# Softmax attention on one Trainium2 core: products of P and V read 232 columns in place of 256

## The chip, the cores and the metric

The kernel runs on one core of a Trainium2 chip. The metric is the device time of one execution in microseconds (us). Before the change it is 2531.12 us, the median of three runs that lie between 2529.14 and 2533.62 us.

## The reference

Two layers work on 1040 frames (16 learned ones and 1024 of the input) of width 1024. Each layer normalises, projects to a group of four gated-linear-attention heads and a group of eight softmax-attention heads of width 64, normalises both outputs by head, projects them back and adds them; then comes a gated feed-forward part with a short causal convolution. The change touches the softmax heads alone:

```python
c = jnp.cumsum(log_f, axis=1)
logits = einsum('bqhd,bkhd->bhqk', q_b * dh ** -0.5, kf) + c_b[..., None] - c_k[:, :, None, :]
logits = jnp.where(key_pos[None, :] <= q_pos[:, None], logits, -jnp.inf)
out = einsum('bhqk,bkhd->bqhd', jax.nn.softmax(logits, axis=-1), vf)
```

Everything is float32. The kernel keeps most operands of its matmuls as two parts, a rounded high one (`hi`, type float32r) and the rest (`lo`), and adds the products of the parts.

## The kernel before

The softmax attention is in `fox` (L770). The 1040 frames are cut into nine tiles: tile 0 has 112 frames (`FIRST`), the others 116 (`FT`). The eight heads are worked on as four pairs `p`, each with two heads `e`. For each pair the query tiles come in the groups (7, 8), (5, 6), (3, 4), (1, 2) and (0). One step of `fox` is one query tile of one head, and steps are laid out in slots:

- `fox_scores` (L644) multiplies queries with keys in up to three stretches of keys (460, 464 and 116 columns; L659 with the high part of the keys, L660 with the low one) into score buffers `S`, of which there are three. VectorE adds the gate's bias and takes the running minimum (L662), ScalarE takes the exponential into `P` (L674).
- Two slots later `fox_transposes` (L681) turns blocks of P on TensorE (L695; L688 for the ninth key tile), and `split` (L336 on ScalarE, L337 on VectorE) writes the high and low parts into `PT`. `PT[0]` holds key tiles 0 to 3, `PT[1]` key tiles 4 to 7, each as 4 places of 232 columns: the two query tiles of the group side by side. Key tile t stands at place `p = 3 - t % 4`, so key tiles 0 and 4 stand last.
- Three slots later `fox_av` (L699) multiplies V with PT into one buffer `av` (L721), 128 rows (high and low part of V, 64 each) by the group's 232 columns. Each key tile gives two matmuls, with the high and the low part of PT, and the same 116 x 128 (or 112 x 128) block of V as the stationary operand. Key tiles that only the later query tile may see are multiplied with 116 columns.
- Later slots fold the two halves of `av` (`fo`, L734), normalise, and store.

Between these steps `work.run` puts matmuls of other work as a filling: the projections of the next head pair and the gate branch (`mm`, L222 to L224, 348 or 344 columns), and for the last pair the output projection (`mm` of 256, 384 and 400 columns). How much goes into a slot is set by `mm_us` (L132), a cost for each matmul that doesn't change here. Within attention the order on each engine is then set by a scheduler, which goes by the order in the program, by its own costs of the instructions, and by a priority that `fox` gives to the scores (L818). In the feed-forward part the order on TensorE is written out by hand.

Of the kernel before, what the change touches and what calls it, by code (L numbers as in the profile page):

```python
# [33 lines left out]
FT, NT, FIRST = 116, 9, 112  # L34
# [101 lines left out]
class Kern:  # L136
# [562 lines left out]
    def fox_av(self, e, tiles, q, PT, avs, pp, part):  # L699
        nc = self.nc  # L700
        if part == 0:
            PT["av"] = pp.tile([128, 256], F32, tag="av", name="av")
        av = PT["av"]
        last = tiles[-1]
        width = FT * (len(tiles) - 1) + self.rows_of(last)
        ts = list(range(4 * part, min(4 * part + 4, last + 1)))
        if part == 0 and last:
            ts[:2] = 1, 0
        for t in ts:
            a, b = 0 if t <= tiles[0] else FT, width  # L710
            for i in range(2):
                if t == NT - 1:
                    w, x = q["Vm"][:, e, :, :], PT[2][:, i, :]
                else:
                    r, p = self.rows_of(t), 3 - t % 4
                    w, x = q["V"][e][:r, t, :, :], PT[part][:r, i, p, a:width]
                    if a == 0 and p < 3:

                        b = 256
                        x = PT[part][:r, i].rearrange("p a b -> p (a b)")[:, 2 * FT * p:2 * FT * p + b]  # L720
                nc.tensor.matmul(av[:, a:b], w.rearrange("p a b -> p (a b)"), x,  # L721
                                 start=(t == ts[0] and part == 0 and i == 0), stop=(t == last and i == 1))
        if last < 4 * part + 4:
            nc.scalar.copy(avs[:, e, :width], av[:, :width])
# [1024 lines left out]
```

## Time and profile before

| | before |
|---|---|
| time, median of three runs | 2531.12 us |
| the profiled execution's own time | 2528.19 us |
| its span, first to last instruction | 2526.4 us |
| mean granted clock of TensorE | 0.996 |
| TensorE busy | 2488.1 us |
| VectorE, ScalarE, GpSimd busy | 1767.5, 1274.1, 381.4 us |
| products of P and V, first and last start over both layers | 189.5 and 1753.7 us |

A row of the groups reads: line, engine, operation, what it writes and reads, rows times columns of the stationary operand, rows times columns of the moving one, count, then busy time in us, mean of one in ns, and idle time before it. A row of the timeline reads: start in us, duration, engine, line, operation, names, shape, how many follow each other under the same names, with the shape of the first; in brackets the idle time before it. A row of stretches reads: from and to, length, busy time and count of each engine in the order that the text names, granted clock, share of the DMA engines, GB/s.

### The profile page before, as it was taken

The numbers are of one execution on the slowest core, as the hardware profiler recorded it, in microseconds if no ns is written. First come the engines' busy times: TensorE is split into PE (matmuls) and PEld (weight loads), VectorE is DVE, ScalarE is ACT, GpSimd is POOL, SyncE is SP. The second block draws the span as 40 slices with busy tenths as digits, with TensorE's granted clock in tenths as the row PEclk, the third lists the DMA queues.
The fourth block names the chain that finished last, engine by engine and source line by source line (L and its number), as shares of the span: only waits on it lengthen the run. The fifth ranks groups of instructions, "written<-read, shape, count | busy, mean of one in ns | idle before, by whom it ended". The sixth has DMA issues, their size and how long they took to land.

```text
span 2526.4 us, 47023 instructions
## 1 busy us (share of the span) xinstructions
PE 2488.1 (98%) x18454; PEld 2386.5 (94%) x18454; DVE 1767.5 (70%) x3515; ACT 1274.1 (50%) x2731; POOL 381.4 (15%) x561
## 2 busy tenths in 40 slices
PE   9999999999999999999999999999999999999998
PEld 8989999999999999999999899999999999997786
DVE  8656777769877777853666666777797777777545
ACT  7346666645544445641443466665464444455412
POOL 1023433110000000100200333431100000001002
PEclk9999999999999999999999999999999999999999
DMA  3232124342322224763312222243432222258622
GB/s 131 68 87 73 50 89 132 116 139 76 118 81 81 81 76 138 196 176 102 105 56 70 74 80 69 67 147 110 145 92 93 76 82 83 77 158 191 183 75 73
DMA packets 117933, 259.75 MB, mean 103 GB/s; under 512 B 14816, under 2 KB 32480, under 8 KB 117712
## 3 DMA queue, kind: packets, MB, share of 16 engines
q1 hardware_dynamic: 93408, 181.74, 23.1%
q0 software_dynamic: 22432, 72.71, 10.4%
q8 instruction: 144, 2.36, 0.4%
q10 hardware_dynamic: 1872, 2.31, 0.3%
q14 instruction: 77, 0.63, 0.1%
HBM read 176.11 MB, written 67.81 MB: 97 GB/s over the span
## 4 chain that ended last, share of the span: by engine, by line
PE 83%; DVE 10%; ACT 4%; issue 1%; DMA 1%; SPq 0%; DVEq 0%; ACTq 0%
PE up L224 11%; PE up L222 11%; PE up L223 11%; PE mm L222 7%; PE mm L224 7%; PE mm L223 7%; PE down L222 5%; PE down L223 5%; PE down L224 5%; PE av L721 3%; PE tr L695 2%; DVE S L662 1%; PE S L659 1%; PE wo L222 1%; PE wo L224 1%
## 5 line engine op out<-in xcount | busy, mean ns | idle before, releaser
L224 PE MATMUL up<-x,hi 128*128 128x260 f32 (+1 forms) x2464 | 698.0, 283 | 2.8 <-DVE x L1090 2.8
L222 PE MATMUL up<-x,hi 128*128 128x260 f32 (+1 forms) x2464 | 698.2, 283 | 2.4 <-ACT x L1089 2.4
L223 PE MATMUL up<-x,lo 128*128 128x260 f32 (+1 forms) x2464 | 697.1, 283 | 0.0
L224 PEld LDWEIGHTS up<-x,hi 128*128 128x128 f32 x2464 | 466.8, 189 | 5.1 <-DVE x L1090 4.8
L222 PEld LDWEIGHTS up<-x,hi 128*128 128x128 f32 x2464 | 465.7, 189 | 3.3 <-ACT x L1089 3.2
L223 PEld LDWEIGHTS up<-x,lo 128*128 128x128 f32 x2464 | 466.0, 189 | 0.1
L1066 DVE TENSOR_TENSOR lo<-raw,hi 128x512 fp32r<-128x512 f32 x364 | 247.5, 685 | 172.0 <-ACT hi L1065 172.0
L222 PE MATMUL mm<-xh,hi 128*128 128x348 f32 (+4 forms) x1056 | 363.6, 344 | 0.0
L224 PE MATMUL mm<-xl,hi 128*128 128x348 f32 (+4 forms) x1056 | 339.6, 322 | 0.0
L223 PE MATMUL mm<-xh,lo 128*128 128x348 f32 (+4 forms) x1056 | 338.9, 321 | 0.0
L1065 ACT CAST hi<-raw 128x512 fp32r<-128x512 f32 x364 | 224.8, 620 | 141.5 <-PE up L224 93.0
L222 PEld LDWEIGHTS mm<-xh,hi 128*128 128x128 f32 x1056 | 199.6, 189 | 5.9 <-issue 5.3
L223 PEld LDWEIGHTS mm<-xh,lo 128*128 128x128 f32 x1056 | 199.5, 189 | 0.4 <-issue 0.3
L224 PEld LDWEIGHTS mm<-xl,hi 128*128 128x128 f32 x1056 | 198.4, 188 | 0.4 <-issue 0.3
L189 ACT CAST hi<-raw 128x512 fp32r<-128x512 f32 (+2 forms) x168 | 97.3, 580 | 183.2 <-PE down L224 108.0
L223 PE MATMUL down<-ah,lo 128*128 128x260 f32 (+1 forms) x528 | 169.1, 320 | 0.0
L222 PE MATMUL down<-ah,hi 128*128 128x260 f32 (+1 forms) x528 | 168.6, 319 | 0.0
L224 PE MATMUL down<-al,hi 128*128 128x260 f32 (+1 forms) x528 | 168.4, 319 | 0.0
L674 ACT ACTIVATE P<-S,m 116x460 f32<-116x460 f32 (+2 forms) x224 | 124.7, 561 | 71.6 <-DVE m L662 67.6
L337 DVE TENSOR_TENSOR PT<-tr,PT 116x464 fp32r<-116x464 f32 (+3 forms) x240 | 122.8, 514 | 47.0 <-ACT PT L336 45.4
L1048 DVE TENSOR_TENSOR raw<-raw,raw 128x512 f32<-128x512 f32 x198 | 129.4, 683 | 18.1 <-DMA raw<-in_wd_dram 15.6
L1279 POOL DMA_DIRECT2D actd<-cv x44 | 23.6, 535 | 763.0 <-DVE cv L1278 742.1
(285 smaller groups left out, 5615.6 us busy)
## 6 DMA issues: line engine op xcount, KB each, us to landing
raw<-in_wm_dram SPq DMA_DIRECT2D x326, 256.0 KB, 2.7
raw<-in_wd_dram SPq DMA_DIRECT2D x64, 256.0 KB, 3.8
actd<-cv POOLq DMA_DIRECT2D x22, 520.0 KB, 3.0
actd<-cv POOLq DMA_DIRECT2D x22, 512.0 KB, 3.0
cb<-cd SPq DMA_DIRECT2D x16, 520.0 KB, 4.2
st<-actd SPq DMA_DIRECT2D x14, 520.0 KB, 5.0
st<-actd SPq DMA_DIRECT2D x14, 512.0 KB, 4.8
kA<-kA SPq DMA_DIRECT2D x24, 260.0 KB, 4.1
```

The source lines that it names most:

```text
L189: nc.scalar.copy(hi[:, :n, :], raw[:, :n, :])
L222: nc.tensor.matmul(ps, wh, xh[:, c0:c0 + n], start=first, stop=False, skip_group_check=more)
L223: nc.tensor.matmul(ps, wl, xh[:, c0:c0 + n], start=False, stop=False, skip_group_check=more)
L224: nc.tensor.matmul(ps, wh, xl[:, c0:c0 + n], start=False, stop=last, skip_group_check=more)
L337: nc.vector.tensor_tensor(out=lo, in0=src, in1=hi.bitcast(F32), op=ALU.subtract)
L659: nc.tensor.matmul(S[:rows, :n], q["qA"][e][:, qs], q["kA"][e][:, c0:k1], start=True, stop=False)
L674: nc.scalar.activation(P[:rows, :n], S[:rows, :n], AF.Exp, scale=-1.0, bias=m[:rows, nch - 1:nch], accum_out=(den if nch == 1 else d3[:row ...
L695: nc.tensor.transpose(tr[:w, 3 - j, :rows], P[:rows, o:o + w], id_)
L721: nc.tensor.matmul(av[:, a:b], w.rearrange("p a b -> p (a b)"), x, start=(t == ts[0] and part == 0 and i == 0), stop=(t == last and i == 1))
L1048: nc.vector.tensor_tensor(out=q[out][:, :nk, :], in0=q[a][:, :nk, :], in1=q[b][:, :nk, :], op=op)
L1065: nc.scalar.copy(hi[:, :nk, :], src[:, :nk, :])
L1066: nc.vector.tensor_tensor(out=lo[:, :nk, :], in0=src[:, :nk, :], in1=hi[:, :nk, :].bitcast(F32), op=ALU.subtract)
```

## The change

Where a product reads both query tiles' columns (`a == 0`) of a key tile that doesn't stand last in PT (`p < 3`), the kernel before reads 256 columns in place of 232. The 24 additional ones are the beginning of the next place of PT; their products land in columns 232 to 255 of `av`, which nothing reads. After the change, every such product reads the 232 columns that it needs.

```diff
                 else:
                     r, p = self.rows_of(t), 3 - t % 4
                     w, x = q["V"][e][:r, t, :, :], PT[part][:r, i, p, a:width]
-                    if a == 0 and p < 3:
-
-                        b = 256
-                        x = PT[part][:r, i].rearrange("p a b -> p (a b)")[:, 2 * FT * p:2 * FT * p + b]
                 nc.tensor.matmul(av[:, a:b], w.rearrange("p a b -> p (a b)"), x,
                                  start=(t == ts[0] and part == 0 and i == 0), stop=(t == last and i == 1))
```

## The prediction

> **What bounds the kernel now.** I read four views: the page's first part for how full each engine is, its chain for which engine sets the end, the table by stretches for the two attention stages that the change touches, and the waits of TensorE there.
>
> ```profile
> span 2526.4 us, 47023 instructions
> ...
> PE 2488.1 (98%) x18454; PEld 2386.5 (94%) x18454; DVE 1767.5 (70%) x3515; ACT 1274.1 (50%) x2731; POOL 381.4 (15%) x561
> ...
> PE 83%; DVE 10%; ACT 4%; issue 1%; DMA 1%; SPq 0%; DVEq 0%; ACTq 0%
> ```
> ```profile
> 188.00:502.00 314.00, 309.40 (x2177) 298.83 (x2177) 224.68 (x712) 204.63 (x619) 105.21 (x158) 0.99 0.30 92
> 1440.00:1756.00 316.00, 311.48 (x2188) 300.28 (x2187) 225.72 (x716) 206.41 (x624) 105.33 (x158) 0.99 0.31 92
> ```
> ```profile
> PE mm L224 <- DVE ml L337: 1.7, 1, 1.7
> PE S L659 <- ACT P L674: 1.3, 3, 0.7
> PE av L721 <- ACT PT L336: 0.3, 1, 0.3
> PE av L721 <- DVE PT L337: 0.3, 1, 0.3
> PE tr L695 <- DVE PT L337: 0.3, 1, 0.3
> ```
>
> TensorE is busy for 98% of the span and holds 83% of the chain that ended last. In the two attention stages (second fence; the columns behind the length are TensorE, its weight loads, VectorE, ScalarE and GpSimd) it is busy 309.4 of 314 us and 311.5 of 316 us, while VectorE and ScalarE are busy 65 to 72% of the time. The third fence, the waits of the first attention stage from 188 to 480 us, adds up to under 4 us, and only 0.6 us of them stand before a product of P and V. So a nanosecond taken from TensorE's stream in these stages is a nanosecond off the end, unless a wait takes its place.
>
> **The change part by part.** It removes columns, and no instruction. In the table of groups, with shapes kept apart, the products of P and V with 128 columns of V stand in these three widest forms:
>
> ```profile
> L721 PE MATMUL av<-PT,V 116*128 116x256 f32 x448 | 96.7, 291 | 0.7 <-ACT PT L336 0.7
> L721 PE MATMUL av<-PT,V 112*128 112x232 f32 x128 | 24.8, 275 | 0.0
> L721 PE MATMUL av<-PT,V 116*128 116x232 f32 x64 | 13.5, 288 | 0.5 <-DVE PT L337 0.5
> ```
>
> The first row is what changes: 448 matmuls read 256 columns and will read 232, like the 192 of the two rows below (those of the first key tile of each four, `p = 3`, which have nothing behind them to read). In the built program of the changed kernel all 640 have 232. The mean of one (291 ns against 275 and 288) is latency and overlaps its neighbours; what a matmul costs is the distance from its start to the next start. The timeline gives it where eight stand together, two of 232 columns and then six of 256. Each run below is quoted as its start, the start of its third matmul, and the start of what follows:
>
> ```profile
> 270.54 1.10 PE L721 MATMUL av<-PT,V 116*128 116x232 f32 x8
> 270.76 0.87 PE L721 MATMUL av<-PT,V 116*128 116x256 f32 x6
> 271.47 0.26 PE L695 MATMUL tr<-ident,P 116*116 116x116 f32 x1
> 281.06 1.10 PE L721 MATMUL av<-PT,V 116*128 116x232 f32 x8
> 281.28 0.88 PE L721 MATMUL av<-PT,V 116*128 116x256 f32 x6
> 281.99 0.26 PE L695 MATMUL tr<-ident,P 116*116 116x116 f32 x1
> 352.18 1.10 PE L721 MATMUL av<-PT,V 116*128 116x232 f32 x8
> 352.41 0.88 PE L721 MATMUL av<-PT,V 116*128 116x256 f32 x6
> 353.12 0.26 PE L695 MATMUL tr<-ident,P 116*116 116x116 f32 x1
> ```
> ```profile
> 278.91 0.28 PE L721 MATMUL av<-PT,V 116*128 116x256 f32 x1
> 279.03 0.38 PE L660 MATMUL S<-kL,qA 128*116 128x460 f32 x1
> 279.25 0.28 PE L721 MATMUL av<-PT,V 116*128 116x256 f32 x1
> 279.37 0.26 PE L695 MATMUL tr<-ident,P 116*116 116x116 f32 x1
> ```
>
> Six of 232 take 0.22 + 0.22 + 0.23 = 0.67 us, 0.112 us each. Eighteen of 256 take 3 x 0.71 = 2.13 us, 0.118 us each; single ones (second fence) take 0.12. The difference is 0.0066 us by the runs and 0.0083 by the singles. A wider lever is the slope over columns, from the output projection's matmuls of 256 and 384 columns:
>
> ```profile
> 457.20 0.27 PE L222 MATMUL mm<-mh,hi 128*128 128x256 f32 x1
> ...
> 458.14 0.27 PE L224 MATMUL mm<-ml,hi 128*128 128x256 f32 x1
> ...
> 472.24 0.33 PE L222 MATMUL mm<-mh,hi 128*128 128x384 f32 x1
> ...
> 473.28 0.34 PE L222 MATMUL mm<-mh,wl 128*128 128x384 f32 x1
> ```
>
> From 457.20 to 458.14 stand eight intervals of 256 columns, 0.1175 us each; from 472.24 to 473.28 six of 384, 0.1733 us each. That is 0.436 ns a column, so 24 columns would be 10.5 ns. Over 448 matmuls the three prices are 3.0, 3.7 and 4.7 us. I take 7.8 ns, 3.5 us, between the first two, since these rows are of the very instruction; 4.7 us stays as the far end and nothing as the near one.
>
> Against this saving speaks the weight load that goes with each matmul. The rows above put a product of 232 columns at 0.112 us. [...]
>
> What moves: the instructions are the same, but the scheduler sees shorter matmuls and orders anew. Of 18,131 rows of TensorE 38 stand elsewhere, 128 of 3,517 on VectorE, 64 of 2,506 on ScalarE, 10 on GpSimd and 2 on SyncE (two loads of the gate branch that change places with a weight load, in a queue that TensorE waits for nowhere in the fence of waits). On TensorE nearly all of it is one place, the first query pair of head pair 0, once a layer: seven projection matmuls (`mm`, 348 columns) that stood between products and transposes now come behind them, ahead of the fold. On VectorE and ScalarE a split of transposed P or a score reduction steps past one or two neighbours. This is where a new wait can come from, so I look at that stretch:
>
> ```profile
> 189.50:204.20 14.70, 13.15 (x97) 11.73 (x95) 10.30 (x33) 11.36 (x35) 3.59 (x6) 1.00 0.00 1
> ```
> ```profile
> 194.00:198.00 4.00, 2.97 (x22) 1.00 0.00 0
> ```
> ```profile
> 205.56 0.32 PE L222 MATMUL mm<-xh,hi 128*128 128x348 f32 x1
> 205.72 0.32 PE L223 MATMUL mm<-xh,lo 128*128 128x348 f32 x1
> ```
>
> TensorE idles 14.70 - 13.15 = 1.55 us there, 1.03 of it between 194 and 198 us, where it waits for the softmax (scores for a free score buffer). A projection matmul takes 0.16 us. If the stretch is held by the softmax chain, the seven no longer fill its holes and come on top: 7 x 0.16 = 1.12 us a layer. If it is held by TensorE, moving them costs nothing; and two of them sat where the new order has products with their operands ready, which could shorten the idle time by as much. ScalarE is busy 11.36 of 14.70 us there, TensorE 13.15, so I take the latter, at nothing, and keep 2 x 1.12 = 2.2 us on either side. VectorE's and ScalarE's steps past a neighbour are hidden by the projection matmuls that stand between a transpose and the product that reads it; where these are gone is the stretch just priced.
>
> The sum: -3.5 + 0 = -3.5 us. The profiled execution took 2528.2 us (its span 2526.4 and 1.8 around it) and would take 2524.7; it lies 2.9 us under the median of the three runs, 2531.1, from which the forecast is 2527.6.
>
> **The rivals.** First, the clock makes it more. In both layers TensorE loses half its clock shortly after its longest wait:
>
> ```profile
> 454.60:458.40 3.80, 2.05 (x18) 1.85 (x18) 3.80 (x16) 3.80 (x12) 0.26 (x1) 1.00 0.21 71
> 458.40:461.80 3.40, 3.40 (x19) 3.40 (x18) 3.40 (x11) 3.40 (x10) 0.97 (x3) 0.50 0.52 155
> ```
>
> After 1.75 us of idleness in 3.8 us the granted clock is 0.50 for 3.4 us, a loss of 1.7 us. [...] Against it: nothing makes the wait itself shorter.
>
> Second, the other side. The first query pair becomes a longer hole: the seven matmuls no longer fill it, 1.12 us are added, and the 1.03 us of idleness between 194 and 198 us become 2.15. That is more than the 1.75 us after which the clock fell, so the clock falls there too, 1.7 us. Twice, once a layer: 2 x (1.12 + 1.7) = 5.6 us, less 3.5: 2533.2, slower than before. It decides from 1.75 us of idleness in about 3.8 us; 0.7 us must come from the new order. For it speaks that this stretch holds the largest waits for the softmax; against it, that the order brings products of P and V forward into the same holes. [...]
>
> Third, the change doesn't do what it says in time: the weight load (94% busy in the page's row) sets the distance, and fewer columns bring nothing. Then 2531.1. The runs of 232 and 256 above speak against it, by 6.6 ns; it would need a load that ends later when all eight are narrow.
>
> **How the numbers follow.** Forecast 2527.6 with 0.62; the clock's gain, 2524.2, 0.14; the hole, 2533.2, 0.14; no effect, 2531.1, 0.10. A measurement of this kernel can tell about 0.2%, 5 us, from no change, so the bounds are 2526.1 and 2536.2. Faster by more: the clock's case, and some 0.08 of the forecast, by the far price of 4.7 us and a little from the order: 0.22. Slower by more: a third of the hole's case, if it spreads to the next query pair: 0.05. Within: 0.73. The range runs from 2523.0 (4.7 + 3.4 us gained) to 2533.2 (the hole); beyond lie only a chance of 0.1 or so. The runs before alone spread from 2529.1 to 2533.6.
>
> **What would show it.** In the groups after, the form of 256 columns is gone and 232 stands at 640. A run of eight takes 8 x 0.112 = 0.89 us from its start to the next transpose, where it took 0.93 or 0.94; if it still takes 0.93, the third rival is right. The two attention stages end 1.7 us earlier each. In the stretch of the first query pair the idle time stays within 0.4 to 2.7 us and the granted clock at 1.00; over 2.7 and under 1.00 the second rival is right. The clock's two falls after the wait for `ml` either stay (forecast) or go (first rival). Wrong would be the forecast if the sum of TensorE's waits in an attention stage grew by over 1.7 us, since then the columns saved are given back.

## The result, and the profile after

The changed kernel takes **2554.32 us** (median of five runs, 2552.75 to 2555.22) against 2531.12 us before (five runs, 2529.14 to 2533.62). The ratio is 1.0089 with a 95% interval of 1.0079 to 1.0100: 23 us slower, where 3.5 us faster was forecast, and 21 us above the range. The profiled execution took 2552.75 us, its span is 2550.9.

The page of the changed kernel, first part and chain:

```profile
span 2550.9 us, 47013 instructions
...
PE 2488.7 (98%) x18454; PEld 2382.9 (93%) x18454; DVE 1773.0 (70%) x3515; ACT 1275.5 (50%) x2731; POOL 381.9 (15%) x561
...
PE 65%; issue 16%; DVE 12%; ACT 5%; DMA 1%; POOL 0%; SPq 0%; DVEq 0%; POOLq 0%; ACTq 0%
```

TensorE's busy time is what it was (2488.7 us against 2488.1), so the 24.5 us that the span gained are not work. In the chain TensorE's share falls from 83% to 65%, but no more should be read into that: 15 of the 18 points go to "issue", time for which the profile shows no wait, and the run e1 below, which is faster than the kernel before, has a chain with 50% TensorE and 30% issue. The stages of attention show where the time goes. The first rows are the changed kernel's two stages and the first query pair, in the columns known from before:

```profile
188.00:512.00 324.00, 308.74 (x2168) 295.72 (x2168) 226.34 (x710) 204.93 (x617) 105.37 (x158) 0.99 0.29 90
1452.00:1776.00 324.00, 308.22 (x2173) 295.73 (x2173) 226.50 (x711) 204.90 (x617) 105.57 (x158) 0.99 0.29 89
189.50:204.20 14.70, 12.19 (x89) 10.73 (x89) 10.31 (x33) 11.37 (x35) 3.57 (x6) 1.00 0.01 2
```

Each stage is some 11 us longer for the same work: 15.3 us of 324 are idle, where before 4.6 of 314 were. The waits of TensorE in the first stage, of the changed kernel (line, what is waited for, us in total, times, longest; from 717 on its lines are four less than before, so L717 is the product):

```profile
PE tr L695 <- DVE PT L337: 8.6, 9, 1.6
PE S L659 <- ACT P L674: 3.4, 4, 1.3
PE mm L224 <- DVE ml L337: 1.8, 1, 1.8
PE av L717 <- DVE PT L337: 0.9, 2, 0.7
```

The transposes of P wait 8.6 us for VectorE's split (0.3 before), the score matmuls 3.4 us for a free score buffer (1.3 before). The groups of the changed kernel show what is waited for:

```profile
L695 PE MATMUL tr<-ident,P 116*116 116x116 f32 x688 | 120.8, 268 | 18.2 <-DVE PT L337 18.0
L717 PE MATMUL av<-PT,V 116*128 116x232 f32 x512 | 100.6, 282 | 1.6 <-DVE PT L337 1.6
```

512 products of 116x232 and, as before, 128 of 112x232: the 256 are gone. A run of eight products of the changed kernel:

```profile
272.53 1.05 PE L717 MATMUL av<-PT,V 116*128 116x232 f32 x8
273.43 0.26 PE L695 MATMUL tr<-ident,P 116*116 116x116 f32 x1
```

It takes 0.90 us where it took 0.93 or 0.94. So the saving is there, matmul by matmul, and something else costs some seven times as much.

**Where the wait is made.** One of the transposes' waits, at the same place of both programs. First before: VectorE and ScalarE between the fold of one query pair and the transposes of the next.

```profile
227.15 0.52 DVE L662 CUSTOM_DVE_ANT_0 S<-S,cb 116x344 f32<-116x344 f32 x1
...
227.61 0.53 ACT L336 CAST PT<-tr 116x464 fp32r<-116x464 f32 x1
...
228.04 0.55 ACT L674 ACTIVATE P<-S,m 116x344 f32<-116x344 f32 x1
...
228.49 0.49 DVE L749 TENSOR_TENSOR fon<-ff,fy 116x128 f32<-116x128 f32 x2
...
228.90 1.01 DVE L337 TENSOR_TENSOR PT<-tr,PT 116x464 fp32r<-116x464 f32 x2
...
229.67 0.56 PE L695 MATMUL tr<-ident,P 116*116 116x116 f32 x4
```

Then the changed kernel:

```profile
228.57 0.17 DVE L279 SCALAR_TENSOR_TENSOR fa<-fy 116x4 f32<-116x4 f32 x1 [0.51 <-ACT fy L278]
...
229.16 0.49 DVE L745 TENSOR_TENSOR fon<-ff,fy 116x128 f32<-116x128 f32 x2
...
229.57 0.52 DVE L662 CUSTOM_DVE_ANT_0 S<-S,cb 116x344 f32<-116x344 f32 x1
...
230.18 0.55 ACT L674 ACTIVATE P<-S,m 116x344 f32<-116x344 f32 x1 [1.64 <-DVE m L662]
...
230.72 0.54 ACT L336 CAST PT<-tr 116x464 fp32r<-116x464 f32 x1
...
231.29 0.64 DVE L337 TENSOR_TENSOR PT<-tr,PT 116x464 fp32r<-116x464 f32 x1 [1.14 <-ACT PT L336]
...
231.98 0.61 PE L695 MATMUL tr<-ident,P 116*116 116x116 f32 x4 [1.38 <-DVE PT L337]
```

Before, the score reduction stands ahead of the fold's last steps on VectorE, and on ScalarE the cast of transposed P stands ahead of the exp. After, both pairs are turned round. The fold has to wait for ScalarE between its steps (0.51 us in the first line), so the reduction comes late; the exp waits 1.64 us for it; the cast, whose operands have long been there, stands behind that exp; the split's second half waits for the cast; and the transposes wait 1.38 us for the split, which frees their buffer. This recurs in every head pair (1.38, 1.37, 1.38 and 1.64 us in the first stage), and a like one stands twice a stage at the score matmuls, some 0.98 us each.

**Theory:** the time comes from the order on VectorE and ScalarE that the scheduler makes for 232 columns, and from the waits that it puts on TensorE; the columns themselves save about what was forecast. **Rivals:** a product of under 256 columns is dear in itself; or the move of TensorE's projection matmuls in the first query pair alone makes the loss; or the moves cost only when they meet. The programs as built bear on the first point: with 232, 236, 240, 244, 248 or 252 written in place of 256, the orders of TensorE and ScalarE come out as in the changed kernel, and with 256 as before. So the order turns between 252 and 256, not gradually. Of these widths 232, 252 and 256 were run, and their traces show it.

### The profile page after: what moved, and what is told of

It reads as the page before. It is cut to its first block, busy times and chain, and to the rows that moved or that the text cites. A ratio compares the mean times of both kernels' runs of the same rounds, so it can differ in the third digit from the quotient of the medians.

```text
span 2550.9 us, 47013 instructions
## 1 busy us (share of the span) xinstructions
PE 2488.7 (98%) x18454; PEld 2382.9 (93%) x18454; DVE 1773.0 (70%) x3515; ACT 1275.5 (50%) x2731; POOL 381.9 (15%) x561
## 4 chain that ended last, share of the span: by engine, by line
PE 65%; issue 16%; DVE 12%; ACT 5%; DMA 1%; POOL 0%; SPq 0%; DVEq 0%; POOLq 0%; ACTq 0%
PE mm L222 7%; PE mm L223 7%; PE mm L224 7%; PE up L222 5%; PE up L224 5%; PE up L223 5%; PE down L222 5%; PE down L223 5%; PE down L224 5%; PE av L717 2%; PE tr L695 2%; DVE S L662 2%; ACT P L674 1%; PE wo L222 1%; PE wo L224 1%
## 5 line engine op out<-in xcount | busy, mean ns | idle before, releaser
L695 PE MATMUL tr<-ident,P 116*116 116x116 f32 x704 | 125.0, 268 | 18.2 <-DVE PT L337 18.0
```

What stands on the lines that cost most here:

```text
L695: nc.tensor.transpose(tr[:w, 3 - j, :rows], P[:rows, o:o + w], id_)
```

## The experiments

In the table the length of an attention stage is the distance in the trace from the start of its first score matmul to the start of its last product. Ratios are to the kernel before, run alongside on the same chip (its medians there: 2532.53 us for the first four, 2532.13 for the next four, 2531.88 for the last two). A stage can hold one short fall of the clock (to 0.50 for 3.4 us), in some runs and not in others; the last section shows what that is worth, so a difference of well under 1 us between two stages is not read.

| run | order made for | columns run | time, us | ratio (95%) | stages, us |
|---|---|---|---|---|---|
| before | 256 | 256 | 2531.12 | 1 | 325.41, 325.15 |
| after | 232 | 232 | 2554.32 | 1.0089 (1.0079 to 1.0100) | 336.66, 336.24 |
| e1 | 256 | 232 | 2528.72 | 0.9986 (0.9978 to 0.9995) | 324.40, 324.40 |
| e2 | 232 | 256 | 2557.04 | 1.0091 (1.0078 to 1.0105) | 337.53, 337.05 |
| e3 | 232 in tiles 3, 4 | 232 | 2542.69 | 1.0037 (1.0024 to 1.0050) | 331.00, 330.70 |
| e4 | 232 in tiles 7, 8 | 232 | 2536.00 | 1.0018 (1.0009 to 1.0027) | 328.07, 328.14 |
| e5 | e3, casts first | 232 | 2533.68 | 1.0011 (1.0002 to 1.0019) | 326.93, 326.54 |
| e6 | 232, casts first | 232 | 2544.81 | 1.0051 (1.0039 to 1.0064) | 332.17, 331.34 |
| e7 | 232 in tiles 5, 6, 1, 2 | 232 | 2536.48 | 1.0017 (1.0008 to 1.0026) | 328.30, 327.73 |
| e8 | 252 | 252 | 2559.74 | 1.0118 (1.0102 to 1.0133) | 338.69, 338.76 |
| e9 | 232, splits raised | 232 | 2563.38 | 1.0130 (1.0112 to 1.0147) | 340.97, 341.28 |
| e10 | 232, scores raised | 232 | 2557.29 | 1.0096 (1.0080 to 1.0112) | 337.65, 337.42 |

### e1 and e2: order and columns taken apart

The width that the scheduler sees and the width that runs are made different: once the program stands in its order with all its waits, the 448 products get another number of columns. e1 is the kernel before with

```diff
+def set_columns(nc, old, new):
+    from copy import replace
...
+    def cut(i):
...
+        x, w = i.ins
+        if w.memref.startswith("Vm") or x.offset % 232 or x.offset % 928 >= 696 or tuple(x.ap[1]) != (1, old):
+            return i
...
+        x, y = (replace(z, ap=[z.ap[0], (1, new)], bass_ap=None) for z in (x, i.outs[0]))
+        return replace(i, ins=[x, w], outs=[y])
+    for f in nc.m.functions:
+        for b in f.blocks:
+            b.instructions = [cut(i) for i in b.instructions]
...
     with _tile.TileContext(nc) as tc:
         tile_hybrid_trunk_kernel(tc, *args)
+    set_columns(nc, 256, 232)
```

and e2 is the changed kernel with `set_columns(nc, 232, 256)`.

> The order of before, with 232 columns: the program is ordered with 256 columns, and the same 448 products of P and V are then cut to 232 with the order and every wait left as they are. Theory (the time comes from the new order on VectorE and ScalarE, the columns themselves save what the forecast said): 2526.4 to 2528, which is 2531.1 less 3.5 to 4.7 us, and TensorE's idle time stays at some 28 us. First rival (a product of under 256 columns costs more in itself, wherever it stands): about 2554, as the changed kernel. Second rival (the columns save nothing, the weight load sets the distance): 2531.

> The reverse: the order of the changed kernel, with the 448 products widened again to 256 columns after the ordering. Theory: 2554.3 plus 3.5 to 4.7 us, 2557.8 to 2559, a little less if some of the added columns fall beside waits (52 us of TensorE's idle time are spread over 2551). First rival (the narrow form itself is dear): 2531.

e1 took 2528.72 us, 0.9986 of before (0.9978 to 0.9995), 0.7 us over what the theory gave; e2 took 2557.04, 1.0091, 0.8 us under it and not to be told from the changed kernel's 1.0089 by the times. By the stages the 24 columns are worth 1.8 us in the old order (650.56 to 648.80) and 1.7 us in the new one (674.58 to 672.90). The order is worth 24.1 us at 232 columns and 24.0 at 256. So the theory holds for the order, and the narrow product is not dear. e1 is also the version that beats both kernels, by its median; its profiled execution alone (2528.37 us against 2528.19) does not show it.

That the stages of e1 gain 1.8 us and not 3 or more is seen in its waits (first stage of e1):

```profile
PE tr L695 <- DVE PT L337: 2.3, 4, 1.2
```

Four waits at the transposes where before had one of 0.3 us. Three are 0.3 to 0.4 us, one in each of the first three head pairs: TensorE is at the transposes sooner and the split is not. The fourth is told of in the last section. So TensorE's idle time, which the theory had staying, grew: span less busy time went from 38.3 to 44.7 us.

TensorE's order is the same in both traces, so they can be laid side by side matmul by matmul. From start to next start a product takes 7.5 ns less in e1 (440 of the 448, those that no wait and no fall of the clock touches); between e2 and the changed kernel, whose orders agree too, it is 8.1 ns (436). Over both stages of e1 the products save 3.3 us. Another 3.2 us go because the clock fell once in each stage before (458.4 and 1711.1 us) and in neither of e1. Longer waits give 3.9 us back, and small shifts elsewhere 0.8, which leaves the 1.8.

### e3, e4 and e7: the new order in parts

The scheduler's answer is local, so it can be had for one group of query tiles at a time: only there does it see 232 columns; elsewhere it sees 256, and all are cut to 232 afterwards. e3:

```diff
-                    if a == 0 and p < 3:
+                    if a == 0 and p < 3 and (tiles[0] != 3):
...
+    set_columns(nc, 256, 232)
```

e4 has `tiles[0] != 7` there, e7 `tiles[0] not in (1, 5)`.

> All 448 products have 232 columns, but the order is that of a program in which only the query pair of tiles 3 and 4 had 232 when it was ordered. Against the order of before this moves, eight times (four head pairs, two layers), one score reduction of 116x344 behind five steps of the fold on VectorE, and two casts of transposed P behind an exp on ScalarE; TensorE's order is that of before. Theory that these moves are the larger cost: the transposes wait 8 x 1.38 = 11 us for the split, so 2527.6 + 11 = 2538.6, with waits of about 1.4 us each at TensorE's transposes. Rival (the cost is in the other moves, or in all together): within 2 us of the old order with 232 columns, 2526 to 2529.

> All 448 products have 232 columns, but the order is that of a program in which only the query pair of tiles 7 and 8 had 232 when it was ordered. Against the order of before this holds the projection matmuls' move in the first query pair (the forecast's second rival), and on VectorE the two score reductions of 116x460 and 116x348 behind steps of the fold and of a gate, once a head pair. Theory: the score matmuls wait some 1 us in two or three head pairs a layer, 4 to 8 us in all: 2531 to 2536. Rival (the moves in the first query pair alone make the loss): over 2545. Rival (this part costs nothing): 2526 to 2529.

> All 448 products have 232 columns, but the order is that of a program in which only the query pairs of tiles 5 and 6 and of 1 and 2 had 232 when it was ordered: what the third and fourth runs left out. Theory, if the parts add: the changed kernel lies 25.6 us over the old order, the parts for 3 and 4 and for 7 and 8 are 14.0 and 7.3, so 4.3 remain, 2531.5 to 2535. Rival (the loss that remains comes only when all parts meet): 2527 to 2530.

Against e1, e3 takes 14.0 us more by the times and 12.9 by the stages. Its order differs from that of e1 in the reduction and the casts, and in the last head pair in a split that also moves behind the fold, all on VectorE and ScalarE; TensorE's is the same. So this part is settled: turning round those neighbours makes the wait. First stage of e3:

```profile
PE tr L695 <- DVE PT L337: 8.2, 8, 1.9
```

The eight waits at this place in both layers (1.39, 1.36, 1.38, 1.92 us in the first, 1.35, 1.37, 1.38, 1.90 in the second) add up to 12.05 us; the forecast of 11 had left out that the last head pair's are longer. The rival, nothing from this part, is out.

e4 takes 7.3 us more than e1 by the times, 7.4 by the stages, within what the theory expected. First stage and first query pair of e4:

```profile
PE S L659 <- ACT P L674: 3.4, 4, 1.3
PE tr L695 <- DVE PT L337: 2.3, 3, 1.2
```
```profile
189.50:204.20 14.70, 12.16 (x89) 10.56 (x88) 10.31 (x33) 11.36 (x35) 3.58 (x6) 1.00 0.01 2
```

The first query pair, with the projection matmuls moved, idles 2.54 us where e1 idles 1.59 in the same stretch, and the clock stays at 1.00. Its whole cost is a little more than these 0.95 us, since the moved matmuls come behind the stretch: where the two orders have met again (e1's projection matmul at 205.43 us), e4 is 1.3 us behind, and as much in the second layer. The prediction's hole was there, then, but without the clock's fall it makes 2.6 us and not 5.6, and not the 23. Most of the rest of e4 is the score matmuls' wait in the next head pairs, 0.94 to 1.00 us each, four in all. By the trace it is made like the other one, by two reductions behind steps of the fold; no run puts these two back by themselves. In the changed kernel:

```profile
274.17 0.16 DVE L279 SCALAR_TENSOR_TENSOR fa<-fy 112x2 f32<-112x2 f32 x1 [0.70 <-ACT fy L278]
...
274.24 0.64 DVE L662 CUSTOM_DVE_ANT_0 S<-S,cb 116x460 f32<-116x460 f32 x1
...
275.37 0.58 DVE L662 CUSTOM_DVE_ANT_0 S<-S,cb,m 116x348 f32<-116x348 f32 x1
...
276.05 0.64 ACT L674 ACTIVATE P<-S,m 116x460 f32<-116x460 f32 x1 [1.04 <-DVE m L662]
...
276.83 0.46 PE L659 MATMUL S<-kA,qA 128*116 128x460 f32 x1 [0.98 <-ACT P L674]
```

VectorE stands 0.70 us before a fold step that waits for ScalarE, with a reduction behind it that had all it needed.

e7, the groups left over, was expected to bring 4.3 us over e1 and brought 7.8 (7.2 by the stages), in waits at the transposes of the first and the last head pair; which of its moves makes them was not tested. First stage of e7:

```profile
PE tr L695 <- DVE PT L337: 3.8, 6, 1.2
```

The parts add up to 12.9 + 7.4 + 7.2 = 27.5 us of stage, the whole is 24.1. So they add nearly; 3.4 us overlap, and the rival that the loss comes only when all moves meet is out.

### e5 and e6: the cast put back in front of the exp

Sixteen times an exp of 116x344 and the cast behind it change places on ScalarE, with the waits that belong to each; the split that waits for the cast then waits for one count less. VectorE and TensorE stay as they are. e5 does this to e3, e6 to the changed kernel.

```diff
+            pairs = [(k, l) for k, l in zip(act, act[1:])
+                     if type(L[k]).__name__ == "InstActivation" and type(L[l]).__name__ == "InstTensorCopy"
+                     and L[k].outs[0].memref.startswith("P_") and tuple(L[k].outs[0].ap[1]) == (1, 344)
+                     and L[l].outs[0].memref.startswith("PT0")]
...
+            for k, l in pairs:
+                L[k], L[l] = L[l], L[k]
```

> The order of the third run (narrow for tiles 3 and 4), with one thing undone: the 16 casts of transposed P that stood behind an exp of 116x344 on ScalarE are put in front of it again, neighbour for neighbour. VectorE keeps the score reductions behind the fold. Theory (TensorE's transposes wait because the cast, and so the split, stands behind an exp whose reduction comes late): the eight waits of 1.35 to 1.92 us go, and the time comes back from 2542.7 to that of the old order, 2527 to 2531. Rival (the late reduction costs by itself, through the late exp and the score buffers): the time stays over 2538, with the waits moved to the score matmuls or the products.

> The changed kernel itself with the same 16 swaps of neighbours on ScalarE and nothing else. Theory, if the parts add: 2554.3 less the 14.0 us between the third and the first run, 2538 to 2543. Rival (the parts don't add, another late step takes over where the cast no longer waits): over 2546.

e5 took 2533.68 us, 9.0 less than e3 and 5.0 more than e1 (stages: 8.2 less, 4.7 more), which is neither what the theory said nor what the rival did. Its timeline at the place of the 1.38 us wait:

```profile
228.62 0.53 ACT L336 CAST PT<-tr 116x464 fp32r<-116x464 f32 x1
...
229.75 0.52 DVE L662 CUSTOM_DVE_ANT_0 S<-S,cb 116x344 f32<-116x344 f32 x1
...
230.19 0.64 DVE L337 TENSOR_TENSOR PT<-tr,PT 116x464 fp32r<-116x464 f32 x1
...
230.37 0.55 ACT L674 ACTIVATE P<-S,m 116x344 f32<-116x344 f32 x1 [1.21 <-DVE m L662]
```

The exp is as late as it was (1.21 us for the reduction), but the cast starts 1.13 us ahead of the reduction, where in the changed kernel it starts 1.15 us behind it, and the split follows the reduction at once. The six waits of the first three head pairs fall from 1.35 to 1.39 us to 0.10 or less. What stays is one wait in each layer's last head pair, 1.48 and 1.50 us, where the split on VectorE itself stands behind the late reduction and the fold, and some 0.3 us a head pair (in the first stage the same transposes of two head pairs are 81.78 us apart, in e1 81.45). So the cast behind the exp is the larger link, about two thirds of this part; the late reduction keeps the last third.

e6 took 2544.81 us, 9.5 less than the changed kernel (9.4 by the stages), about as much as e5 brought, and not the 14.0 expected. It lies between the two ranges: the part adds and no other step takes over, but the swap undoes only the cast's share.

### e8: 252 columns

```diff
-                        b = 256
+                        b = 252
```

> Before's kernel with 252 columns written in place of 256, and so ordered by the scheduler. The order that comes out is that of the changed kernel on TensorE and ScalarE, and within 36 rows of it on VectorE. Theory (the order makes the time, four columns a product are worth under 1 us): 2552 to 2558. Rival (the time goes with the columns): at most a sixth of the way from 2531.1 to 2554.3, 2530 to 2535.

It took 2559.74 us, 1.0118 (1.0102 to 1.0133): slower than with 232. Four columns fewer turn the order round and cost more than 24 do. First stage of e8:

```profile
PE tr L695 <- DVE PT L337: 9.7, 8, 2.0
PE S L659 <- ACT P L674: 4.8, 4, 1.7
```

The time goes with the order and not with the columns. It lies 1.7 us above the range expected: the score matmuls' recurring wait is 1.65 to 1.69 us a time, four times in both layers, where the changed kernel has 0.98, which is 2.8 us; VectorE's order differs from that kernel's in 36 rows.

### e9 and e10: priorities in place of the old order

```diff
-        self.split(PT[ci][:w, 0, at, qs], PT[ci][:w, 1, at, qs], tr[:w, at, :rows])
+        with self.tc.high_priority(16):
+            self.split(PT[ci][:w, 0, at, qs], PT[ci][:w, 1, at, qs], tr[:w, at, :rows])
```

is e9; e10 has `high_priority(16)` in place of `high_priority(8)` around the scores.

> The changed kernel with the splits of transposed P raised by 16 places for the scheduler, nothing else written differently. In the order that comes out no score reduction of 116x344 or 116x460 stands behind the fold on VectorE any more, while the 16 casts still stand behind an exp on ScalarE; TensorE's order changes in 390 rows. Theory (the late reduction is what makes the exp late, and the cast behind it waits for that): the waits of 1.4 us at the transposes and of 1.0 us at the score matmuls go, 2532 to 2542. Rival (a cast behind an exp is late whatever the reduction does): no less than 2550. Rival (the moved rows of TensorE open waits of their own): anywhere over 2542, with the waits at other products than before.

> The changed kernel with the score steps raised by 16 places in place of 8 for the scheduler. The reductions of 116x344 and 116x460 again stand ahead of the fold, eight of the 16 casts stand behind an exp, and TensorE's order changes in 534 rows. Theory: as for the raised splits, 2532 to 2542. Rival (the moved rows of TensorE open waits of their own): over 2542.

Both miss: 2563.38 and 2557.29 us, slower than the changed kernel or no better. The wait at the old place shrinks as the theory says (in e9 to 0.43 to 0.47 us in the first three head pairs, with the reduction ahead of the fold and the cast still behind the exp; in e10 to 0.22 to 0.25), but the order that comes out opens others. First stage of e9:

```profile
PE S L659 <- ACT P L674: 5.2, 4, 1.8
PE tr L695 <- DVE PT L337: 4.4, 8, 1.0
PE av L718 <- DVE PT L337: 3.0, 7, 0.8
```

The rival with waits of its own was right in both; in e10 the score matmuls wait eight times, 4.8 us, and the products six times for the split, 2.4 us.

## Why the prediction was wrong

- **What bounds the kernel:** right before, no longer after. "A nanosecond taken from TensorE's stream in these stages is a nanosecond off the end, unless a wait takes its place" held with its second half.
- **The price of the columns** (7.8 ns each, 3.5 us): right as a price, 7.5 and 8.1 ns in the two orders, and the run of eight takes 0.90 us where 0.89 was to show it. As a gain it is 1.8 us of stage in e1, since part of it comes back as waits before transposes; by the times of e1 it is 3.5 us, with an interval of 1.3 to 5.6. The rival without any effect is out.
- **The first query pair** (0, at most 2.2 us either way): it costs 1.3 us a layer, 2.6 in all, with the clock at 1.00. The bound was nearly good and the value in it wrong: the softmax chain holds this stretch, not TensorE. As a cause of the result it is small.
- **The step that failed** is the sentence "VectorE's and ScalarE's steps past a neighbour are hidden by the projection matmuls that stand between a transpose and the product that reads it; where these are gone is the stretch just priced." The 128 and 64 moved rows were counted, and put at nothing outside one stretch. What hides a late split is not only the time to the product that reads it: the split also frees the buffer that the transposes two places further on write to (8.6 us of waits in the changed kernel's first stage), and the exp frees a score buffer (3.4 us). These waits have no projection matmul left in front of them. In their place the runs showed 12.9 us for the reduction behind the fold with the cast behind the exp, 7.4 us for the two reductions behind fold and gate with the first query pair's 2.6 in it, and 7.2 us for the rest, 24.1 together. Of the first of the three a swap undid two thirds (e5), so its cause is shown; in the other two the cause is read from the waits.
- **Which rival:** none. The second had the right sign and kind, a hole made by the new order, but put it on TensorE's moved rows. Its hole was priced well, 1.12 us a layer against 1.3, but its step to the clock was wrong: the changed kernel idles 14.70 - 12.19 = 2.51 us in this stretch at a clock of 1.00. The first rival, the clock's gain, is out too: no run shows the 3.4 us (twice the 1.7 us of a fall) that its 2524.2 us and the range's fast end, 2523.0, count on. The changed kernel has both falls, at 464.7 and 1734.4 us, and in e1, where both are gone, most of the 3.4 us comes back as two waits, of 1.25 and 1.23 us.
- **The prediction's own test** named this outcome: TensorE's waits in a stage growing by over 1.7 us. They grew by about 11. The chance for it was too small because no rival was made of the moves on VectorE and ScalarE, though their rows were there to be looked at one by one: in the two places shown above, the instruction that is now in front still has to wait for another engine.

## What to carry to other kernels

Where a scheduler orders the program, a change of an operand's size is a change of order, and the moved rows have to be read on every engine: look for an instruction with its operands ready that now stands behind one that waits, and follow which buffer it frees. To find out which of the two a change is, run the old order with the new sizes and the new order with the old sizes; here one pair of runs split the 23 us lost into some 24 to 26 lost by the order and 2 to 4 saved by the columns. A price at nothing for "steps past a neighbour" needs the same bound from both sides as any other term.

## What the runs showed of the hardware

The clock's falls don't follow from the length of the wait alone. Before, the clock fell to 0.50 for 3.4 us after a stretch of 3.8 us with 1.75 idle. In e1 the same place, with 1.80 us idle, is followed by the full clock:

```profile
453.40:457.20 3.80, 2.00 (x18) 1.80 (x17) 3.80 (x16) 3.80 (x12) 0.26 (x1) 1.00 0.25 71
457.20:460.60 3.40, 3.15 (x27) 2.90 (x25) 3.40 (x11) 3.40 (x10) 0.98 (x3) 1.00 0.52 157
```

Nor do the falls follow from the idle time just ahead of them alone. In the 3.41 us ahead of its falls the kernel before idles 1.75, 1.66, 1.75 and 1.87 us, and 3.41 at the program's end; the changed kernel 1.80, 1.95 and 1.88 us, and 2.87 at the end. But the changed kernel also idles 1.66 us from 1751.49 to 1754.90 us and 1.67 us from 2400.02 to 2403.43 us, and keeps the full clock both times. What else counts, no run here shows.

The falls stand at regular distances. Those ahead of the program's end last 3.41 us each, and in both traces they start whole multiples of 3.413 us apart: in the kernel before at 458.37, 611.97 (45 multiples later), 1711.06 (367) and 1864.66 us (412), in the changed kernel at 464.66, 1734.42 (372) and 1888.02 us (417). What makes them so, no run shows.

And a fall is not always lost time. At a clock of 0.50 for 3.4 us it should cost 1.7 us, an estimate from these two figures. But in e1, without it, TensorE comes earlier to a transpose at 461.59 us and waits 1.25 us there for the split, a wait that the kernel before doesn't have. e5 has both cases in one execution: the first stage has the fall (459.66 us) and no such wait, the second has no fall and waits 1.22 us at the same transposes (1718.99 us), and the first stage is only 0.4 us longer (326.93 against 326.54). In e6 and e7, which also have a fall in the first stage alone, that stage is 0.8 and 0.6 us longer. So most of the 1.7 us of a fall is hidden here, behind a split that comes no sooner.
